# A state space and attention trunk on one core: both mixings reordered, the state space operators on VectorE, small products by turns on column parts

## The chip, the cores and the metric

The kernel runs on one core of one Trainium2 chip. The metric is the device time of one execution in microseconds; three runs of the kernel before are given, and one further execution was taken with the hardware profiler. Engines are named as in the profile: PE (TensorE), with PEld for its weight loads, DVE (VectorE), ACT (ScalarE), POOL (GpSimd) and SP (the queue that issues most DMAs).

## The reference

Two decoder layers over 256 tokens of width 1024, all in float32. Each layer projects the normed tokens with `w_in` into 768 "self" columns and 256 memory queries, mixes them, projects back with `w_out`, and adds a gated MLP with a three-tap causal convolution (1024 to 2 x 2816 to 1024).

- Layer 0 mixes the self columns with a diagonal state space model: 48 groups of 16 channels, 64 complex states each. Discretised operators come from `lambda`, `log_step`, B and C; then GELU, and a sigmoid gate with `w_glu` (768 x 768).
- Layer 1 mixes them by causal attention, 12 heads of 64, over keys and values computed once from the tokens that enter that layer (with 256 tokens the block selection of the reference leaves only the own block).
- In both layers 4 more heads attend without a mask to 256 memory tokens, normed and projected with `w_mem_kv`.

## The kernel before

Activations lie transposed, channels on partitions and the 256 tokens in the free dimension. A weight is loaded by SP in tiles of 128 x 1024 in a fixed list (`Stream`, L64 to L130), then usually split: ACT copies it to a rounded high part (L115), DVE subtracts to get the low part (L119, L121), and each product is three one-pass matmuls (`mm3`, L249 to L251). Weights named in `NATIVE` (L32) are not split; they are multiplied in plain float32. PE executes in program order.

Layer 0 is written as small steps, most of them generators, and a string `ORDER` names them one by one. Inside `manual_schedule` PE, DVE and POOL execute in the order of that string; ACT and SP, and everything after it, are ordered by a scheduler's priorities. In it:

- `P` projects with `w_in` (L869). `rx*`, `rm*` are the norms of tokens and memory: sums of squares on POOL, a power on POOL (L288), a Newton step on DVE.
- `coefficients` (L680 to L745) computes the discretised eigenvalues in many small DVE operations before anything else. `E0`, `E1` raise them to 64 powers in four rounds (piece 0: 8 pairs of groups, on DVE; piece 1: 16 pairs, on POOL).
- The 768 columns are three blocks of 8 pairs. For block b: `Xr`, `Xi` form the input operator (L638: two products of 128 x 512, two sums of 64 x 512), `T`, `t` transpose its halves on PE, `B` copies a part, `V` forms the output operator in three operations of 128 x 1024 (on POOL, L635), `u` scales the projected input, `U` places it by copies (on ACT or DVE, by `U_ACT`).
- `S` is the state recurrence in four steps: products with the input operator on PE (L896, L897), six rotations on DVE, two scans on DVE, then the rotation back into `H` (DVE, partly POOL, L925, L926).
- `l0`, `l1` build the operators inside a chunk on PE (L838, L841), and `L` copies them out. `Y` forms the outputs from both (L941, L944) and transposes them, `G` is GELU.
- `K`, `K1` project the memory for layers 0 and 1 (`mem_kv`, L377, L381). `mkv` of layer 1 is split in three products, and `m` splits the memory tokens for it. `q` scales the memory queries, `A` moves all four memory heads by one stage.

After the string come the gate products with `w_glu`, the gate itself, the output projection and the addition to the tokens (L1079), and then the MLP of layer 0 (`psU`, from 183.07 us of the trace). Layer 1 is ordered by priority throughout; `ORDER1` gives the order in which its steps are issued. A head there is four steps: scores, softmax, transposes, product with the values (L470, L471). The two heads of a pair write the lower and the upper 64 partitions of one bank.

## Time and profile before

| | |
|---|---|
| three runs | 694.43, 694.61, 701.04 us (median 694.61) |
| profiled execution | 695.04 us, of which the span from first to last instruction is 693.3 us |
| busy in the span | PE 654.1 us (94%), DVE 565.4 (82%), ACT 413.2 (60%), POOL 132.9 (19%) |
| mean granted PE clock | 0.957 of 2.4 GHz |
| stages | layer 0 mixing to 183, MLP to 375, layer 1 mixing to 496.7, MLP and final norm to 693.3 us |

PE busy counts an instruction from its start to a modelled end, so neighbours overlap: what one product costs is read from the distance between starts. Plain float32 matmuls show as two records each. A stretch's clock of 0.77 means that PE ran for part of it at 1.2 instead of 2.4 GHz.

### The profile page before, as it was taken

To read this page: it belongs to the slowest core of one execution; us is meant where nothing else is said; L and a number is where in the kernel's file an instruction comes from. 1 tells how busy PE (TensorE), PEld (TensorE's weight loads), DVE (VectorE), ACT (ScalarE), POOL (GpSimd) and SP (SyncE) were. 2 spreads that over 40 slices of the span, in tenths; PEclk is the share of its full clock that TensorE was granted. 3 is DMA by queue.
4 is the path that set the end of the run, shared out by engine and by line. 5 is a ranking of instruction groups with operands and counts; after the bars stand their busy time and mean duration, and the time that the engine had idled before them with its cause. 6 is when DMAs were issued, how large, how long until landed. Compare 5 with 4: busy or idle time off the path is not lost.

```text
span 693.3 us, 12668 instructions
## 1 busy us (share of the span) xinstructions
PE 654.1 (94%) x4904; PEld 616.5 (89%) x4904; DVE 565.4 (82%) x1012; ACT 413.2 (60%) x747; POOL 132.9 (19%) x134
## 2 busy tenths in 40 slices
PE   6369899999999999999999998989999999999995
PEld 5358888998899999999999997868999999999984
DVE  7996999796879998888888798974749999888872
ACT  6368625576556665555557579864636666555631
POOL 5795623402300000000001255500300000000000
PEclk9775879999999999999999999899999999999998
DMA  8610133274455555555555544323625555565401
GB/s 315 245 62 1 61 99 99 93 217 148 152 181 184 183 183 181 186 185 182 182 186 156 168 128 140 107 89 122 213 92 182 181 186 183 183 188 187 172 1 61
DMA packets 43259, 105.13 MB, mean 152 GB/s; under 512 B 3776, under 2 KB 14144, under 8 KB 43200
## 3 DMA queue, kind: packets, MB, share of 16 engines
q1 hardware_dynamic: 42624, 103.74, 45.9%
q8 instruction: 38, 0.62, 0.4%
q10 hardware_dynamic: 576, 0.59, 0.2%
q14 instruction: 21, 0.17, 0.1%
HBM read 103.28 MB, written 1.05 MB: 150 GB/s over the span
## 4 chain that ended last, share of the span: by engine, by line
PE 82%; DVE 12%; DMA 2%; issue 2%; ACT 1%; POOL 0%; SPq 0%; DVEq 0%; ACTq 0%
PE psU L250 12%; PE psU L251 12%; PE psU L249 12%; PE acc L557 9%; PE acc L249 7%; PE acc L250 7%; PE acc L251 7%; PE ps L377 2%; DVE wlo L119 2%; PE ps L381 2%; PE ps L838 1%; DMA s5c<-s5b 1%; PE psO L470 1%; DVE X L638 1%; PE psT L458 1%
## 5 line engine op out<-in xcount | busy, mean ns | idle before, releaser
L115 ACT ACTIVATE whi<-wraw 128x1024 fp32r<-128x1024 f32 (+1 forms) x176 | 182.9, 1042 | 142.4 <-PE psU L250 84.9
L119 DVE TENSOR_TENSOR wlo<-wraw,whi 128x1024 fp32r<-128x1024 f32 (+1 forms) x176 | 217.9, 1240 | 26.7 <-PE acc L251 13.1
L250 PE MATMUL psU<-xlo,whi 128*128 128x256 f32 x704 | 198.6, 282 | 1.4 <-DVE xlo L331 1.4
L251 PE MATMUL psU<-xhi,wlo 128*128 128x256 f32 x704 | 197.8, 282 | 0.0
L249 PE MATMUL psU<-xhi,whi 128*128 128x256 f32 x704 | 197.6, 282 | 0.0
L250 PEld LDWEIGHTS psU<-xlo,whi 128*128 128x128 f32 x704 | 132.9, 189 | 2.5 <-DVE xlo L331 1.8
L249 PEld LDWEIGHTS psU<-xhi,whi 128*128 128x128 f32 x704 | 132.7, 189 | 0.7
L251 PEld LDWEIGHTS psU<-xhi,wlo 128*128 128x128 f32 x704 | 132.6, 189 | 0.0
L528 DVE SCALAR_TENSOR_TENSOR y<-u,held,y 128x254 f32<-128x254 f32 (+1 forms) x176 | 77.8, 477 | 1.5 <-ACT y L526 1.5
L521 DVE TENSOR_TENSOR u<-psU,rb 128x512 f32<-128x512 f32 x44 | 30.3, 688 | 32.4 <-PE psU L251 31.3
L526 ACT ACTIVATE y<-u,held 128x256 f32<-128x256 f32 x88 | 47.6, 589 | 13.0 <-DVE u L521 12.9
L269 POOL TENSOR_TENSOR sq<-sq 128x512 f32<-128x512 f32 x5 | 8.0, 1598 | 226.9 <-DVE held L364 179.1
L251 PE MATMUL acc<-ah,wlo 128*128 128x256 f32 x176 | 49.7, 283 | 0.0
L250 PE MATMUL acc<-al,whi 128*128 128x256 f32 x176 | 49.7, 283 | 0.0
L249 PE MATMUL acc<-ah,whi 128*128 128x256 f32 x176 | 49.6, 282 | 0.0
L869 PE MATMUL acc<-xg,wraw 128*128 128x256 f32 x128 | 34.1, 429 | 5.5 <-ACT xg L859 5.5
L869 PEld LDWEIGHTS acc<-xg,wraw 128*128 128x128 f32 x128 | 27.7, 221 | 10.0 <-ACT xg L859 5.5
L288 POOL TENSOR_TENSOR y<-mf,held 128x1 f32<-128x1 f32 x2 | 1.1, 550 | 180.5 <-DVE mf L1215 180.5
L249 PEld LDWEIGHTS acc<-ah,whi 128*128 128x128 f32 x176 | 33.6, 191 | 0.0
L251 PEld LDWEIGHTS acc<-ah,wlo 128*128 128x128 f32 x176 | 33.5, 191 | 0.0
L250 PEld LDWEIGHTS acc<-al,whi 128*128 128x128 f32 x176 | 33.5, 191 | 0.0
L250 PE MATMUL acc<-xlo,whi 128*128 128x256 f32 x112 | 31.7, 284 | 0.0
(271 smaller groups left out, 1475.1 us busy)
## 6 DMA issues: line engine op xcount, KB each, us to landing
wraw<-w_up SPq DMA_DIRECT2D x88, 512.0 KB, 3.4
wraw<-w_down SPq DMA_DIRECT2D x44, 512.0 KB, 3.4
wraw<-w_out SPq DMA_DIRECT2D x16, 512.0 KB, 3.6
wraw<-w_in SPq DMA_DIRECT2D x15, 512.0 KB, 3.5
wraw<-w_mem_kv SPq DMA_DIRECT2D x8, 512.0 KB, 4.2
wraw<-w_kv SPq DMA_DIRECT2D x6, 512.0 KB, 3.7
wraw<-w_kv SPq DMA_DIRECT2D x8, 384.0 KB, 3.4
wraw<-w_glu SPq DMA_DIRECT2D x6, 384.0 KB, 3.5
```

The lines of the kernel that those rows point to most:

```text
L115: self.nc.scalar.activation(hi[:, c], t[:, c], AF.Copy, scale=1.0 if g_ is None else g_)
L119: self.nc.vector.tensor_sub(lo[:, c], t[:, c], hi[:, c].bitcast(F32))
L249: PE.matmul(out, whi, ahi, start=first, stop=False, skip_group_check=True)
L250: PE.matmul(out, whi, alo, start=False, stop=False, skip_group_check=True)
L251: PE.matmul(out, wlo, ahi, start=False, stop=last, skip_group_check=True)
L377: PE.matmul(pk[:, 256 * m:256 * m + 256], w[i][:, o + 128 * m:o + 128 * m + 128], g[j], start=k + m + i + j == 0, stop=k == KT - 1, skip_g ...
L381: PE.matmul(pv[:, 256 * t:256 * t + 256], g[j][:, 128 * t:128 * t + 128], w[i][:, o + 256:o + 512], start=k + t + i + j == 0, stop=k == KT ...
L521: V.tensor_mul(u, v2(p), rb2(rb))
L526: S.activation(y[:, j], u[:, j], AF.Identity, bias=cp(3), scale=cp(2))
L528: V.scalar_tensor_tensor(y[:, j, d:], u[:, j, :T - d], cp(2 - d), y[:, j, d:], op0=ALU.mult, op1=ALU.add)
L557: PE.matmul(dacc[2 * t + h], a_, w_[:, 512 * i:512 * i + 512], start=False, stop=last and a_ is al, skip_group_check=True)
L869: PE.matmul(acc[2 * h + b][:, 256 * (m % 2):256 * (m % 2) + 256], w[:, 512 * i + 128 * m:512 * i + 128 * m + 128], xg[k // 2][:, k % 2], s ...
```

## The change

1. `V` runs on DVE but for the last of its nine operations (`V_POOL`), all of `H` on DVE, `Xr2` instead of `Xi0` on POOL. The rounds of the powers are shared out singly: POOL has the last of piece 0 and the first three of piece 1. Copies move between ACT and DVE (`U_ACT` leaves 4 of 12 DVE copies, `T_ACT`, `Y_ACT`, `EVAC_ACT`).
2. The state products use 64 columns of weights at a time, lower and upper half by turns (`tile_position`); the chunk operators go round four column parts of 32; the outputs alternate between two of 64; and the two heads of a pair are multiplied with their values by turns, in a step of their own (`p`).
3. `mkv` of layer 1 is native: no low parts, no split memory (`m` is gone), four passes instead of three. The skip term's operands come ready from memory, so the DVE products `dd` go.
4. Both strings are new. Layer 0's has a `|`: what stands behind it (gate, output projection and the addition are steps now: `g`, `g0` to `g2`, `o`, `z`) goes by priority. `P` moves in half steps, softmax in two. The list of weights follows the strings (`by_steps`).

```diff
-NATIVE = (("mkv", 0), ("win", 0))
+NATIVE = (("mkv", 0), ("mkv", 1), ("win", 0))
...
-P rm0 E0 P rx1 E1 P rx2 E0 P rx3 Xi0 Xr0 E0 V1 u0 t0 V0 V0 Xi1 u1 P B0 T0 D0 V0 Xr1 V1 U1 U0 P U0 l0 U0 T1 E1 U0 E1
-E1 Xi2 Xr2 E0 U1 S0 V1 P t2 S0 T2 S0 L0 U1 L0 P B1 L0 V2 t1 S0 D1 u2 U1 V2 U2 U2 U2 m S1 U2 S2 K S1 K K D2 K rm1 V2
-S1 B2 q l1 S1 L1 L1 rm2 L0 S2 Y0 S2 m S2 K K K K rm3 Y0 K L1 L1 G0 m K1 Y1 G0 Y2 Y1 K1 K1 m Y2 K1 G1 G2 K1 K1 G1 K1
-A G2 A A A A K1 A K1 A
+P E0 P P E1 P P P rm0 E0 Xr0 rx1 P P P rx2 E0 rx3 E0 E1 P Xi0 u0 D0 P U0 T0 U0 P U0 t0 P E1 D2 Xr1 P U0 V0 B0 Xi1 S0
+u1 V0 V0 l0 T1 Xi2 U1 S0 P U1 S0 l0 V2 V1 P V1 L0 V2 t1 K Xr2 B1 S0 L0 T2 U1 K u2 V1 rm1 U2 K U2 U1 L0 L0 Y0 B2 K U2
+t2 U2 E1 S1 V2 l1 D1 l1 l1 l1 L1 rm2 L1 S1 rm3 S2 Y0 S1 S1 K L1 K S2 K S2 Y0 L1 S2 K K1 Y1 K G0 G0 | q Y2 Y2 h1 Y1 h2
+Y1 h1 h3 h3 K1 K1 h0 Y2 h2 G1 h1 G2 h0 K1 K1 h0 K1 G1 h2 G2 h3 h1 h2 h0 K1 h3 K1 g g g g g p1 g0 g0 g g1 p0 g1 p1 K1
+g2 p0 o o o o g2 o o o o z3 z2 z1 z0
 """
-X_POOL = ((0, 1),)
-E_POOL = (1,)
-M_POOL = (1, 2, 3)
-H_DVE = (1,)
-V_DVE = ()
-Y_ACT = (0, 1, 2)
-EVAC_ACT = (0, 1, 2)
-T_ACT = ((0, 0), (0, 1), (1, 0), (1, 1), (2, 0), (2, 1))
-U_ACT = ((1, 1, 1, 0), (0, 1, 1, 1), (1, 0, 1, 1))
+V_POOL = ((2, 2),)
+X_POOL = ((2, 0),)
+E_POOL = ((0, 3), (1, 0), (1, 1), (1, 2))
+H_DVE = (0, 1, 2)
+Y_ACT = (1,)
+EVAC_ACT = (0, 2)
+T_ACT = ((0, 0), (0, 1), (1, 1), (2, 0), (2, 1))
+U_ACT = ((1, 1, 1, 0), (1, 1, 1, 1), (1, 1, 1, 1))
 ORDER1 = """
-I I r1 X I I I r2 X I I I r3 Q0 qm Q1 h0 Q2 Q1 h2 K h0 K K X X h3 h2 K h1 R0 h1 h2 K K v v Q0 R1 R0 h3 R1 h0 h4 h5
-h1 h3 v R2 v h7 e0 h10 Q2 h4 h6 h5 h8 h9 h7 h4 v v v h11 R2 v h2 h10 h6 h9 h13 h4 h5 h1 h14 h8 h6 h10 h0 h8 h12 h6
-h7 h12 h3 O h11 h7 h13 h9 h14 h11 e1 h8 h12 h15 h15 h9 h13 h10 h12 h14 h13 h15 h5 h11 O O h15 h14 O O z1 O O O z0 z2
-z3
+x x x x I I I X r1 r2 I I I I r3 I X Q0 qm Q1 K K Q1 h0 K X h3 X h2 Q2 K h1 h0 K h2 h2 R0 h1 h2 v Q0 R1 v R0 h3 R1 v
+h0 h3 h1 K Q2 h10 h7 h0 h1 h5 v R2 h4 h3 h5 h4 h4 h7 v v h8 h5 h4 h11 h6 h10 h9 v v p0 h6 e0 h9 h10 h6 R2 h13 h5 p1 h7
+h8 h14 h8 h7 h8 h12 h6 p1 p0 e1 h10 h9 h12 O h11 p3 h13 h12 h12 h9 h15 h11 p3 h13 h14 h11 h15 h14 p4 p5 h13 h15 p2 p2
+p5 p4 p6 O h14 O h15 p7 p6 p7 O z0 O O O O z3 z2 z1
 """
-ST_DVE = [('k', 1)]
+ST_DVE = (('k', 1), ('q', 0))
...
+    def by_steps(steps, **lists):
+        its = {n: iter(l) for n, l in lists.items()}
+        return [w for s_ in steps.split() if s_ in its for w in next(its[s_], ())]
...
+    order = by_steps(ORDER, P=[w0[:2], []] + [p for w in w0[2:] for p in ([w], [])], K=mkv(0), K1=mkv(1), g=one(glu),
+                     o=one(wout(0)))
+    order += ffn_order(0)
+    order += by_steps(
+        ORDER1, I=one(win(1)),
+        K=one([(("wk", ks, b), blocks(a["w_kv"], ks, 256 * b, 256), (4, 256)) for ks, b in WK]),
+        v=one([(("wv", ks, c), blocks(a["w_kv"], ks, SELF + 384 * c, 384), (2, 384)) for c in range(2) for ks in PAIRS]),
+        O=one(wout(1)))
+    order += ffn_order(1)
...
+                PE.matmul(pk[:, 256 * m:256 * m + 256], w[:, o + 128 * m:o + 128 * m + 128], mk, start=k + m == 0,
+                          stop=k == KT - 1, skip_group_check=True)
...
+                PE.matmul(pv[:, 256 * t:256 * t + 256], mk[:, 128 * t:128 * t + 128], w[:, o + 256:o + 512],
+                          start=k + t == 0, stop=k == KT - 1, skip_group_check=True)
...
-    def pv(out, off, v, PT, causal):
-        c = 128 if causal else 0
-        PE.matmul(out[off:off + 64, :256], v[0], PT[:, 0], start=True, stop=False, skip_group_check=True)
-        PE.matmul(out[off:off + 64, c:256], v[1], PT[:, 1, c:], start=False, stop=True, skip_group_check=True)
-    def head(h, sl, bs, bt, bo, q, k, v, causal, outp, hi, lo):
+    def pv(out, pair, causal):
+        for t in range(2):
+            c = 128 if t and causal else 0
+            for h in range(2):
+                v, PT = pair[h]
+                PE.matmul(out[64 * h:64 * h + 64, c:256], v[t], PT[:, t, c:], start=t == 0, stop=t == 1,
+                          skip_group_check=True)
+    def head(h, sl, bs, bt, q, k, v, causal, outp):
         p = scores(bs, q(h // 4), k(h // 4), h // 2 % 2, h % 2, causal)
         yield
-        P = softmax(sl, p, causal)
+        m = softmax(sl, p, causal)
+        next(m)
         yield
-        PT = transp(sl, bt, P, causal)
+        P = next(m)
         yield
...
+        outp[h] = v(h), transp(sl, bt, P, causal)
         yield
...
+    def head_pair(i, bo, causal, outp, hi, lo):
+        po = bo("psO")
+        pv(po, [outp.pop(2 * i + h) for h in range(2)], causal)
+        yield
+        o = po[:, :256]
+        S.activation(hi[i], o, AF.Copy)
+        V.tensor_sub(lo[i], o, hi[i].bitcast(F32))
+        yield
...
-            op(v[:, :, 1:5], cb[0], ab[0], ALU.mult)
-            yield
-            op(t, cb[1], ab[1], ALU.mult)
-            yield
-            op(v[:, :, 1:5], v[:, :, 1:5], t, ALU.add)
-            yield
+            for r, (o_, a_, b_, f) in enumerate(((v[:, :, 1:5], cb[0], ab[0], ALU.mult), (t, cb[1], ab[1], ALU.mult),
+                                                 (v[:, :, 1:5], v[:, :, 1:5], t, ALU.add))):
+                (gop if (b, r) in V_POOL else vop)(o_, a_, b_, f)
+                yield
         def local_operator(i):
             n, nf = LEN[i], LEN[i] // 4
             Tm[i] = s5.tile([128, n, 4, 32], F32, name=f"Tm{i}")
             G.memset(Tm[i], 0.0)
...
             for f in range(nf):
+                o = [p[32 * s:32 * s + 32, 128 * f:128 * f + 128] for s in range(4)]
+                for g in range(2):
+                    for s in range(4):
+                        PE.matmul(o[s].rearrange("p (i c) -> p i c", c=32)[:, :, 16 * g:16 * g + 16],
+                                  Bz[i][:, 4 * f + s, g], Vd[i][:, 4 * f + s, g, 0:4], start=g == 0, stop=False,
+                                  tile_position=(0, 32 * s), skip_group_check=True)
                 for s in range(4):
-                    pr = 4 * f + s
-                    o = p[32 * s:32 * s + 32, 128 * f:128 * f + 128]
-                    for g in range(2):
-                        PE.matmul(o.rearrange("p (i c) -> p i c", c=32)[:, :, 16 * g:16 * g + 16],
-                                  Bz[i][:, pr, g], Vd[i][:, pr, g, 0:4], start=g == 0, stop=False,
-                                  tile_position=(0, 32 * s), skip_group_check=True)
...
+                    PE.matmul(o[s][:, :32], ident[:, 32 * s:32 * s + 32], dsk[:, PC[i][0] // 4 + f], start=False,
+                              stop=True, tile_position=(0, 32 * s), skip_group_check=True)
+                yield
...
-                if ks != (0,):
-                    yield
+                    if ks != (0,):
+                        yield
...
-                PE.matmul(pr[:, 64 * j:64 * j + 64], RT[b][0][:, j], U[b][:, j], start=True, stop=True)
-                PE.matmul(pi[:, 64 * j:64 * j + 64], RT[b][1][:, j], U[b][:, j], start=True, stop=True)
+                for ri, p in enumerate((pr, pi)):
+                    for c in HALF:
+                        PE.matmul(p[c, 64 * j:64 * j + 64], RT[b][ri][:, j, c], U[b][:, j], start=True, stop=True,
+                                  tile_position=(0, c.start), skip_group_check=True)
...
+            for s in range(4):
+                o = [py[64 * f:64 * f + 64].rearrange("p (i s c) -> p s i c", s=4, c=32)[:, s] for f in range(2)]
+                for f in range(2):
+                    PE.matmul(o[f], U[b][:, 4 * f + s], Tm[pc][:, off + 4 * f + s], start=s == 0, stop=False,
+                              tile_position=(0, 64 * f), skip_group_check=True)
+                for g in range(2):
+                    for f in range(2):
+                        PE.matmul(o[f][:, :, 16 * g:16 * g + 16], Hs[b][:, 4 * f + s, g],
+                                  Vd[pc][:, off + 4 * f + s, g, 1:5], start=False, stop=True,
+                                  tile_position=(0, 64 * f), skip_group_check=True)
             yield
...
+        def gate():
+            d["g"] = [ba("acc") for _ in range(3)]
+            for ks, b in GLU:
+                gemm(d["g"], ("glu", ks, b), ks, lambda k: [yp[k // 2][i][:, k % 2] for i in range(2)], 2 * b, 2,
+                     ks[0] == 0, ks[0] == 3)
                 yield
+        def gated(b):
+            t = sx([128, 2, T], name="gt")
+            S.activation(t, v2(d["g"][b]), AF.Tanh, scale=0.25)
+            V.scalar_tensor_tensor(t, t, 1.0, yT[b], op0=ALU.add, op1=ALU.mult)
+            yield
...
+        def output0():
+            d["o"] = [ba("acc") for _ in range(4)]
+            yield from gemm_halves(d["o"], "wout", 0, WOUT[0], lambda k: (moh[k - 6], mol[k - 6]) if k >= 6 else
+                                   (oh[k // 2][:, k % 2], ol[k // 2][:, k % 2]))
...
+        by_hand, by_priority = ORDER.split("|")
+        with tc.manual_schedule(engines=MANUAL):
+            steps(by_hand)
+        steps(by_priority)
...
+        for i in range(2):
+            gens[f"p{i}"] = head_pair(i, bank(2), False, outm, ohi[6:], olo[6:])
+        for i in range(6):
+            gens[f"p{2 + i}"] = head_pair(i, bank(5), True, outq, ohi, olo)
```

## Rows read from the trace of the kernel before

**Rows 1.** The page: the span, and PE's granted clock in 40 equal slices.

```profile
span 693.3 us, 12668 instructions
...
PEclk9775879999999999999999999899999999999998
```

**Rows 2.** Busy time by stage: length, PE, PEld, DVE, ACT, POOL; clock, DMA share, GB/s.

```profile
24.00:118.90 94.90, 76.99 (x477) 67.06 (x478) 86.99 (x127) 52.11 (x126) 56.57 (x60) 0.77 0.22 70
118.90:183.00 64.10, 64.10 (x557) 61.15 (x556) 49.48 (x73) 41.54 (x74) 15.92 (x16) 1.00 0.49 160
183.00:190.00 7.00, 5.84 (x49) 5.64 (x49) 7.00 (x9) 4.04 (x7) 3.32 (x3) 1.00 0.41 125
...
418.00:460.00 42.00, 36.31 (x211) 31.08 (x209) 36.96 (x71) 34.90 (x82) 18.16 (x17) 0.88 0.39 128
```

**Rows 3.** Who waited for whom, PE, 0 to 200 us: total, times, longest.

```profile
PE ps L771 <- DVE X L638: 11.8, 1, 11.8
```

**Rows 4.** DVE in order of time: start, length of the merged row.

```profile
32.01 4.62 DVE L638 TENSOR_TENSOR X<-xt 64x512 f32<-64x512 f32 x2
36.66 2.26 DVE L638 TENSOR_TENSOR ee<-E 128x16 f32<-128x16 f32 x1
...
44.18 1.44 DVE L638 TENSOR_TENSOR X<-xt 64x512 f32<-64x512 f32 x2
...
58.34 0.19 DVE L638 TENSOR_TENSOR ee<-E 128x16 f32<-128x16 f32 x1
```

**Rows 5.** POOL in order of time.

```profile
36.16 2.72 POOL L635 TENSOR_TENSOR Vd<-Vd,vt 128x1024 f32<-128x1024 f32 x1
```

**Rows 6.** DVE groups, 24 to 118.9 us: count, busy us, mean ns, idle before.

```profile
L888 DVE COPY U<-uT 32x128 f32<-32x128 f32 x12 | 6.8, 563 | 0.3
...
L121 DVE SCALAR_TENSOR_TENSOR wlo<-wraw,held,whi 128x512 fp32r<-128x512 f32 x4 | 6.0, 1526 | 0.0
...
L903 DVE TENSOR_TENSOR rot<-ps,E 128x512 f32<-128x512 f32 x3 | 2.1, 685 | 4.9 <-PE ps L896 4.9
```

**Rows 7.** DVE groups, 118.9 to 190 us.

```profile
L119 DVE TENSOR_TENSOR wlo<-wraw,whi 128x1024 fp32r<-128x1024 f32 x14 | 17.4, 1246 | 4.8 <-ACT ks L415 1.5 <-PE acc L251 1.4 <-PE ps L381 0.8
```

**Rows 8.** POOL groups, 24 to 118.9 us.

```profile
L635 POOL TENSOR_TENSOR Vd<-Vd,vt 128x1024 f32<-128x1024 f32 x3 | 7.9, 2639 | 0.0
L635 POOL TENSOR_TENSOR Vd<-s5c 128x1024 f32<-128x1024 f32 x3 | 7.0, 2356 | 0.1
L926 POOL TENSOR_TENSOR H<-rot 64x504 f32<-64x504 f32 x4 | 6.3, 1580 | 11.6 <-DVE rot L920 11.5
L635 POOL TENSOR_TENSOR vt<-s5c 128x1024 f32<-128x1024 f32 x3 | 6.2, 2080 | 0.2
```

**Rows 9.** PE in order of time, layer 0.

```profile
43.63 3.62 PE L869 MATMUL acc<-xg,wraw 128*128 128x256 f32 x16
...
80.42 0.39 PE L897 MATMUL ps<-U,RT 128*128 128x64 f32 x2
80.64 0.39 PE L896 MATMUL ps<-U,RT 128*128 128x64 f32 x2
...
101.10 0.41 PE L838 MATMUL ps<-Vd,Bz 128*32 128x64 f32 x4
...
101.61 0.41 PE L838 MATMUL ps<-Vd,Bz 128*32 128x64 f32 x4
...
109.92 0.22 PE L944 MATMUL psY<-Vd,H 128*64 128x64 f32 x1
109.92 0.32 PE L941 MATMUL psY<-Tm,U 128*64 128x128 f32 x1
```

**Rows 10.** PE in order of time, layer 1's value products.

```profile
468.39 0.65 PE L470 MATMUL psO<-PT,vv 128*64 128x256 f32 x2
...
473.75 0.66 PE L470 MATMUL psO<-PT,vv 128*64 128x256 f32 x4
```

**Rows 11.** The chain that ended last: one-pass products of 512 columns.

```profile
669.25 16.78 PE acc L557 x72
```

More of the change, by code (lines that the diff above doesn't have):

```diff
@@ L364, in residual, with mem_kv @@
                 V.scalar_tensor_tensor(xs, accs[b], scale, xs, op0=ALU.mult, op1=ALU.add)
-    def mem_kv(l, bk, mh, ml, ks, new, vm):
+    def mem_kv(l, bk, mem, ks, new, vm):
         pk, pv = bk(), bk()
@@ L370, in mem_kv @@
             if k % 2 == 0:
-                w = W.get(("mkv", l, k // 2))
-            o = 512 * (k % 2)
-            g = [m if m is None else m[k // 2][:, k % 2] for m in (mh, ml)]
-            pairs = [(i, j) for i, j in ((0, 0), (0, 1), (1, 0)) if w[i] is not None and g[j] is not None]
+                w, _ = W.get(("mkv", l, k // 2))
+            o, mk = 512 * (k % 2), mem[k // 2][:, k % 2]
             for m in range(2):
-                for i, j in pairs:
-                    PE.matmul(pk[:, 256 * m:256 * m + 256], w[i][:, o + 128 * m:o + 128 * m + 128], g[j],
-                              start=k + m + i + j == 0, stop=k == KT - 1, skip_group_check=True)
+                PE.matmul(pk[:, 256 * m:256 * m + 256], w[:, o + 128 * m:o + 128 * m + 128], mk, start=k + m == 0,
+                          stop=k == KT - 1, skip_group_check=True)
             for t in range(2):
-                for i, j in pairs:
-                    PE.matmul(pv[:, 256 * t:256 * t + 256], g[j][:, 128 * t:128 * t + 128],
-                              w[i][:, o + 256:o + 512], start=k + t + i + j == 0, stop=k == KT - 1,
-                              skip_group_check=True)
+                PE.matmul(pv[:, 256 * t:256 * t + 256], mk[:, 128 * t:128 * t + 128], w[:, o + 256:o + 512],
+                          start=k + t == 0, stop=k == KT - 1, skip_group_check=True)
             yield
@@ L776, in transpose_input_operator, with powers @@
                     V.tensor_copy(o, p)
-        def powers(i, op):
+        def powers(i):
             e, n = E[i], LEN[i]
-            for c, up, down in ((2, 1, 0), (6, 1, 2), (14, 7, 6), (42, 21, 20)):
+            for r, (c, up, down) in enumerate(((2, 1, 0), (6, 1, 2), (14, 7, 6), (42, 21, 20))):
+                op = gop if (i, r) in E_POOL else vop
                 h = e[:, :, :, c // 2]
@@ L992, in layer0 @@
         acc = [ba("acc") for _ in range(4)]
-        gens = {"P": project(acc), "K": mem_kv(0, bw, memT, None, ks, st, vm),
-                "K1": mem_kv(1, bw, mh, ml, ks1, lambda *_: next(st1), vm1),
-                "E0": powers(0, gop if 0 in E_POOL else vop), "E1": powers(1, gop if 1 in E_POOL else vop),
-                "A": attend([head(h, sq, br, bw, bw, lambda i: qs, lambda i: ks, values_of(vm), False, outp, moh, mol)
-                             for h in range(4)])}
+        gens = {"P": project(acc), "K": mem_kv(0, bw, memT, ks, st, vm),
+                "K1": mem_kv(1, bw, memT, ks1, lambda *_: next(st1), vm1), "E0": powers(0), "E1": powers(1),
+                }
+        for h in range(4):
+            gens[f"h{h}"] = head(h, sq, br, bw, lambda i: qs, lambda i: ks, values_of(vm), False, outp)
+        for i in range(2):
+            gens[f"p{i}"] = head_pair(i, bw, False, outp, moh, mol)
         for b in range(3):
@@ L1050, in layer0, with steps @@
                 calls[f"{n}{b}"] = lambda f=f, b=b: f(b)
+        gens["g"], gens["o"] = gate(), output0()
+        for b in range(3):
+            gens[f"g{b}"] = gated(b)
+        for b in range(4):
+            calls[f"z{b}"] = lambda b=b: residual0(b)
         for i in range(2):
-            calls[f"l{i}"] = lambda i=i: local_operator(i)
+            gens[f"l{i}"] = local_operator(i)
             gens[f"L{i}"] = put_local_operator(i)
-        with tc.manual_schedule(engines=MANUAL):
-            for s in ORDER.split():
+        def steps(text):
+            for s in text.split():
                 if s in gens:
@@ L1091, in layer1 @@
         causal_ops.extend([identb, maskb])
-        act, d = split_x(1), {}
+        sq_, d = [], {}
+        act = split_x(1, steps=sq_)
         rb = pool.tile([128, T], F32, name="rbq")
```

117 lines of the change are left out of this document (30 added, 87 removed).

## The prediction

> **What bounds the kernel now.** The page first: the low digits of PE's granted clock lie in the first seven slices, with one 8 about slice 25 and one at the very end [rows 1]. PE is the engine with most work, so time can be won where it waits or runs slowly. The stage table gives the sizes [rows 2]. From 24.0 us (where the coefficients end) to 118.9 us (where DVE finishes the last step of the third `S`), PE is busy 77.0 of 94.9 us, at a clock of 0.77, while DVE is busy 87.0 of 94.9. From 118.9 to 183.0, where the MLP begins, PE is busy for all of 64.1 us at full clock. So the first stretch is DVE's, the second is PE's. The two MLPs are full on PE and untouched. Layer 1's mixing is full on PE too, except from 418 to 460 us: 36.3 of 42 us at a clock of 0.88.
>
> The list of waits shows how DVE holds PE: 11.8 us at once for the first input operator [rows 3]. Then look at DVE's operations in order of time. An operation of 16 columns (`ee`) takes 2.26 us at 36.66 us and 0.19 us at 58.34; two halves of `X` take 4.62 us at 32.0 and 1.44 at 44.2 [rows 4]. At 36.16 us POOL runs one of the `V` operations for 2.72 us [rows 5], and the slow `ee` ends when that does. DVE is standing in front of something that POOL holds. I set each DVE group of the stretch against its undisturbed duration (0.72 us for 512 columns by the fast `X` halves, 0.19 for `ee`, and so on); the largest single excess is that of the four half tiles of `wlo`, 4 x (1.53 - 0.72) = 3.2 us [rows 4, 6]. Over some fifteen groups I get **24.0 us of delay in DVE's 87.0**; 63.0 us are work. POOL was busy 56.6 us meanwhile, 21.1 of them `V` and 6.3 `H` [rows 2, 8].
>
> **First stretch, DVE's sum.** Taken away: two low part tiles of `mkv`, 4 x 0.72 = 2.9 us; `m` and `dd`, 2.1 (estimate at undisturbed length); `q` moved behind the bar, 2.1; eight `U` copies at about 0.5, 4.0 [rows 6]. Together 11.1. Added: eight `V` operations of 1024 columns; DVE's operation of that size is the split, 1.25 us with some delay in it [rows 7], so I take 1.2, 9.6 us in all. The four halves of `H` from POOL, 4 x 0.68, 2.7; two copies of transposes and one of outputs, 1.8; the round of powers that comes less the one that goes, 1.1. Together 15.2. DVE's work is then 63.0 - 11.1 + 15.2 = 67.1 us. `Xr2` for `Xi0` is even.
>
> Delay: POOL loses eight of nine `V` operations (21.1 - 2.6 = 18.5), `H` (6.3), one subtraction for `m` (1.3) and some 3 of powers, so 56.6 falls to about 27.4 us. At the old rate, 24.0/56.6 = 0.42 us of DVE delay for each us of POOL, 11.6 us remain. Bounds: 4 us, if POOL's rest lies beside DVE operations that read PSUM (the first rotations, `L903`, took 0.685 us on the mean with POOL at work beside the first of them [rows 6]); and 27 us, if all of it holds DVE. I take 11.6, the rate of the rows. Idle: DVE stood 7.9 us, 4.9 of them for the first state products [rows 6], which PE could reach only after `l0`; in the new string `S0` stands ahead of `l0`. Bounds 3 and 8, I take 5.
>
> So the third `S` ends at 24.0 + 67.1 + 11.6 + 5 = 107.7 us, **11.2 us sooner**. PE must keep up. At full clock its old work there takes less than 77.0 us, and it loses there. A group of chunk products and skip term repeats every 0.51 us at full clock, 24 of them 12.3 us [rows 9]. By turns on four column parts it should take half or less: where the old outputs pass from one column part to the other, two products start in the same hundredth of a microsecond [rows 9], and where layer 1's value products of two heads happen to lie side by side, four records take 0.66 us as two do alone [rows 10]. So 5 to 6 us go. The state products, 48 at 0.22 us [rows 9], gain between nothing (if loading 128 columns of weights in two halves takes as long) and half; I take 3 of 10.7. Against it `Y1` (2 us after turns) and one step of `K1` (1.7) come in from the second stretch. About 72 us of PE in 83.7 then: PE hides under DVE, without much to spare.
>
> **Second stretch, PE's sum.** It was 64.1 us of PE without a gap. `Y1` moves ahead of it (8 x 0.455 = 3.65 us by the outputs' own spacing), since `S1` now ends well before `S2`: -3.65. `Y2` by turns: from 3.65 to 2.2 (0.6 of it, as the one overlap in the rows suggests), -1.45. Four memory heads' value products side by side instead of one by one: eight products of 0.43, half of it saved, -1.7. `K1` native: a plain product takes 3.62/8 = 0.45 us less the tail of the last, 0.43 between starts [rows 9], so 32 of them 13.9; before, 96 passes at 0.117 (half of 16.78/72 for 512 columns [rows 11]), 11.3. So +2.6; one of its eight steps lies earlier, -1.7. DVE has work here too (the weights' low parts, GELU, softmax), but was busy only 49.5 of 64.1, and loses the other two low part tiles. The new danger is the gate, which stands in a queue of its own behind `G2`; with heads and `K1` between to fill, I add 1. Sum: 64.1 - 3.65 - 1.45 - 1.7 + 2.6 - 1.7 + 1 = 59.2 us. The MLP begins at 107.7 + 59.2 = 166.9 instead of 183.1: **-16.2 us**. DVE is full from 183 to 190 before and after (the addition, the split of the tokens), so that corner stays.
>
> **Layer 1.** The gap between 418 and 460 us is worth 5.7 us of idle and, by the clock of 0.88, at most 5 more. For it: value products always by pairs (three pairs of heads that lay apart, 0.8 us each, 2.4 us), softmax's multiplication in its own step, one stack of queries off POOL, statistics sooner. Against it: three more steps between a head's scores and its use, so that a buffer stays taken longer, and 1.4 us more on DVE, which was busy 37.0 of 42. I take -4, bounds -9 and +3. Following the weights' list by use and the half steps of `P` I cost at nothing: weights are loaded ahead and PE's order holds the same products; a load that came late would cost PE a wait such as the list of waits does not show now.
>
> The sum: 695.04 - 16.2 - 4 = 674.8 us for the profiled execution, which lies 0.4 above the median; so **674 us**.
>
> **The rivals.** *More than that.* The new string lays POOL's rest out of DVE's way: delay 4, idle 3, the third `S` ends at 98, the MLP begins at 157, layer 1 gives 9: about 660. For it speaks that the operations POOL keeps are short; against, that the powers work only on SBUF, as DVE's `X`, `V` and scans do.
>
> *POOL's rest holds DVE for all its time.* Delay 27 and idle 8: the third `S` ends at 24 + 67.1 + 35 = 126.1, later than now, the MLP begins at 185, and with layer 1's 4 the time is 693, no change. The break-even is plain: delay and idle together may be 33 us, and were 31.9. For it speak [rows 4, 5], where the wait lasted as long as POOL's operation; against, that less than half of POOL's time turned into delay. The Trainium skill, in "SBUF — State Buffer", section "SBUF: two separate sides", says that VectorE operations with two SBUF inputs and GpSimd operations that read SBUF lock one shared pair of ports for the whole instruction, the loser blocking fully. The slow `ee` agrees with that; moving `V` to DVE does not end the lock, it adds eight more operations that want it.
>
> *The turns bring nothing.* If parts of the array load and multiply one after the other, `Y2` and the pairs lose their 3.2 us, and PE's work in the first stretch rises to some 80 of 83.7 us, which would delay DVE's chain by about 4: 681.
>
> *Slower.* PE falls to 1.2 GHz for good in the first stretch: shorter, more scattered products leave it idle more often. Its work there at full clock is about 55 us (half of `P` is done by 24 us); at a mean clock of 0.5 that is 110 us, the third `S` ends at 134, the MLP begins at 193, and with -4 from layer 1 the time is 701. It decides below a clock of 55/83.7 = 0.66; the old string had 0.77 with PE idle for 18 us [rows 2].
>
> **How the numbers follow.** Forecast 0.50 (665 to 684 by half of each bound), more 0.20, POOL holds DVE 0.14, turns bring nothing 0.10, slower 0.06. To leave out no more than 2 in 10 the range must reach from the case above 660 to about 690: 657 to 690. A change under 1% (7 us) can't be told from none here. Faster by more: 0.50 + 0.20 + 0.10 and a fifth of the POOL case, 0.83; slower by more, most of the last case and a little of the POOL case, 0.06; the rest 0.11.
>
> **What would show it.** In the profile after: `V` on DVE at 1.2 us each; the third `S` over near 108 us with DVE over 90% busy up to there; PE full from there to an MLP that starts near 167 us; state products at 0.22 us or less, chunk operators in a quarter to a half of their time; `K1` at 1.73 us a step. The forecast is wrong if DVE's small operations are as slow as before beside POOL's powers, if PE shows gaps after 108 us before the gate's products, or if layer 1's stretch of low clock has grown.

## The result, and the profile after

The changed kernel takes 671.23 us (median of 4 runs, 669.97 to 672.11), the kernel before 694.83 us on the same chip (4 runs, 694.43 to 701.04): a ratio of 0.9639, 95% interval 0.9582 to 0.9696. The profiled execution took 671.97 us. Runs of the kernel before fall near 694.5 or near 700 us, and every ratio carries that spread; the variants are therefore compared with the changed kernel by their own medians and by marks in their traces.

The page first: span, PE and POOL busy in the whole span, PE's granted clock by slices, to be read against [rows 1].

```profile
span 670.2 us, 12678 instructions
...
PE 629.2 (94%) x4968; PEld 595.2 (89%) x4968; DVE 547.5 (82%) x1011; ACT 408.0 (61%) x746; POOL 103.7 (15%) x117
...
PEclk9799698899999999999999997999999999999998
```

The low digits of the first seven slices are fewer, and one low digit stays in layer 1. Now the stage table, with the columns of [rows 2]: up to the end of the third `S`, from there to the first MLP, the MLP's first 7 us, and layer 1's mixing.

```profile
24.00:105.50 81.50, 66.75 (x688) 57.42 (x687) 75.18 (x119) 51.74 (x130) 36.48 (x49) 0.90 0.25 83
105.50:165.50 60.00, 55.42 (x424) 51.78 (x425) 47.88 (x73) 38.70 (x69) 12.65 (x10) 0.91 0.50 174
165.50:172.50 7.00, 7.00 (x60) 6.93 (x59) 6.32 (x11) 4.77 (x8) 2.23 (x2) 1.00 0.01 2
...
354.80:472.40 117.60, 113.32 (x867) 106.60 (x866) 97.68 (x185) 88.89 (x199) 32.60 (x27) 0.96 0.39 129
```

By these marks the first MLP begins 17.6 us sooner (165.5 for 183.1). Layer 1's first projection starts at 354.86 instead of 375.0, so another 2.5 us lie in the first MLP's stretch. The second MLP begins at 472.4 instead of 496.7: 4.2 more for layer 1. The rest is 197.8 us long for 196.6.

The waits of PE, 0 to 200 us (columns as in [rows 3], whose 11.8 us for `X` is gone):

```profile
PE psY L943 <- DVE H L925: 10.3, 3, 8.4
PE acc L866 <- ACT xg L856: 5.5, 1, 5.5
PE ps L286 <- POOL sq L282: 4.8, 2, 3.4
PE psS L431 <- DVE qs L412: 3.0, 1, 3.0
PE ps L834 <- DVE Vd L642: 2.7, 1, 2.7
```

PE still waits for DVE in the first stretch, but inside one place, the first outputs. What DVE does just then, and POOL beside it, each in order of time:

```profile
53.21 0.69 DVE L902 TENSOR_TENSOR rot<-ps,E 128x512 f32<-128x512 f32 x1
...
55.61 0.68 DVE L906 TENSOR_TENSOR rot<-rot 128x512 f32<-128x512 f32 x1
56.21 1.76 DVE L907 TENSOR_TENSOR rot<-rot 128x512 f32<-128x512 f32 x1
57.89 2.28 DVE L910 TENSOR_TENSOR_SCAN rot<-dec,rot 128x512 f32<-128x512 f32 x1
60.10 2.22 DVE L911 TENSOR_TENSOR_SCAN rot<-dec,rot 128x512 f32<-128x512 f32 x1
62.24 2.33 DVE L642 TENSOR_TENSOR Vd<-s5c 128x1024 f32<-128x1024 f32 x2
...
69.74 0.68 DVE L917 TENSOR_TENSOR rot<-rot,E 128x512 f32<-128x512 f32 x1
...
52.71 2.96 POOL L639 TENSOR_TENSOR X<-xt 64x512 f32<-64x512 f32 x2
...
55.93 1.49 POOL L280 TENSOR_TENSOR sq<-sq 128x512 f32<-128x512 f32 x1
57.38 1.71 POOL L281 TENSOR_TENSOR sq<-sq 128x512 f32<-128x512 f32 x1
59.17 2.06 POOL L282 TENSOR_TENSOR sq<-sq 128x512 f32<-128x512 f32 x1
...
69.21 1.79 POOL L828 MEMSET Tm<- 128x2048 f32 x1
```

As in [rows 4, 5], a DVE operation with both inputs in SBUF is long where POOL reads SBUF too: a scan takes 2.2 us here and 1.2 us in the second and third block, where POOL is idle; L907 takes 1.76 us, while its neighbour of the same size, which began before POOL's, takes 0.68. It is not long wherever POOL works: the rotations that read PSUM (from 53.21 us) keep 0.68 us each beside POOL's `X`, and L917 keeps it beside a POOL operation that only writes (`MEMSET`). `V` costs 1.2 us on DVE (two records in 2.33).

The rest of PE's order in time: one block's state products, the chunk operators, the outputs. They answer [rows 9].

```profile
80.73 2.09 PE L895 MATMUL ps<-U,RT 128*64 128x64 f32 x64
82.75 0.43 PE L834 MATMUL ps<-Vd,Bz 128*32 128x64 f32 x16
...
83.06 0.41 PE L834 MATMUL ps<-Vd,Bz 128*32 128x64 f32 x16
...
105.67 0.39 PE L939 MATMUL psY<-Tm,U 128*64 128x128 f32 x4
105.89 0.40 PE L943 MATMUL psY<-Vd,H 128*64 128x64 f32 x8
106.12 0.39 PE L939 MATMUL psY<-Tm,U 128*64 128x128 f32 x4
```

Four pairs of chunk operators now repeat every 0.3 us instead of 4 x 0.51; a block's state products take 2.1 us instead of 16 x 0.22 = 3.5; two pairs of outputs repeat every 0.455 us, which one pair took before (its spacing in the prediction).

### The profile page after: what moved, and what is told of

Its sections match the earlier page's. It is cut to its first block, busy times and chain, and to the rows that moved or that the text cites. A ratio compares the mean times of both kernels' runs of the same rounds, so it can differ in the third digit from the quotient of the medians.

```text
span 670.2 us, 12678 instructions
## 1 busy us (share of the span) xinstructions
PE 629.2 (94%) x4968; PEld 595.2 (89%) x4968; DVE 547.5 (82%) x1011; ACT 408.0 (61%) x746; POOL 103.7 (15%) x117
## 4 chain that ended last, share of the span: by engine, by line
PE 76%; DVE 18%; ACT 2%; issue 2%; DMA 0%; POOL 0%; DVEq 0%; ACTq 0%
PE psU L262 13%; PE psU L260 12%; PE psU L261 12%; PE acc L562 9%; PE acc L261 7%; PE acc L262 7%; PE acc L260 7%; DVE wlo L119 2%; DVE X L642 1%; PE psO L481 1%; DVE xt L642 1%; PE ps L388 1%; DVE cf L649 1%; DVE Vd L642 1%; PE psT L465 1%
## 5 line engine op out<-in xcount | busy, mean ns | idle before, releaser
L119 DVE TENSOR_TENSOR wlo<-wraw,whi 128x1024 fp32r<-128x1024 f32 (+1 forms) x176 | 212.8, 1212 | 31.2 <-PE psU L262 14.9
L262 PE MATMUL acc<-xhi,wlo 128*128 128x256 f32 x112 | 31.6, 283 | 0.0
```

The source lines that it names most:

```text
L119: self.nc.vector.tensor_sub(lo[:, c], t[:, c], hi[:, c].bitcast(F32))
L262: PE.matmul(out, wlo, ahi, start=False, stop=last, skip_group_check=True)
```

## Experiments

Eight kernels start from the changed one, four from the one before (where a string is exchanged, its steps are translated to the new sizes). Beside the medians stand marks of the trace: the end of the third `S` and the start of layer 1's first projection, in the changed kernel 105.5 and 354.9 us, in the one before 118.9 and 375.0. A mark comes from one execution. How far marks scatter shows in the kernel with layer 1's old order: its layer 0 is the changed one, yet the third `S` ends at 106.2 us and the first MLP begins at 163.4, 2.1 us sooner. Differences of this size are not read from marks alone.

### `V` back on POOL

```diff
-V_POOL = ((2, 2),)
+V_POOL = tuple((b, r) for b in range(3) for r in range(3))
```

> The changed kernel with all nine output operator operations on POOL again, as before the change; the strings stay. Theory A (the sum of the prediction): what POOL does costs DVE 0.42 us per us, so eight operations back on POOL (18.5 us) cost DVE 7.8 us of delay and free 9.6 us of its work; moving them was about even and the gain came from elsewhere: 668 to 675 us, as the changed kernel (671). Theory B (the lock is what the change was about): nearly all of the 18.5 us delay DVE, which is the bound up to 105 us, and POOL's queue makes DVE wait for the powers: 680 us or more.

676.0 us (674.94 to 676.59), ratio 0.969 [0.9636, 0.9744], between the two theories; third `S` 114.4, layer 1 at 360.0. DVE's busy time is what my arithmetic made it, 73.0 us for 75.2. But its idle time rises from 6.3 to 17.4 us, and the waits of 24 to 114.4 us, of PE and of DVE, say why:

```profile
PE ps L834 <- POOL Vd L639: 7.1, 1, 7.1
...
DVE RT L780 <- PE ps L775: 11.5, 1, 11.5
```

The chunk operators stand in PE's order and wait for `V`, which comes late through POOL's queue; the transposes that DVE needs stand behind them. **DVE's busy time is no reason for the move: it pays by latency.**

### `V` and `H` on DVE in the kernel before, nothing else

```diff
-H_DVE = (1,)
-V_DVE = ()
+H_DVE = (0, 1, 2)
+V_DVE = (0, 1, 2)
```

> The kernel before with one part of the change alone: all output operator operations and all of the last rotation's sums on DVE, in the old string. Theory A (0.42 us of delay per us of POOL): DVE gets 10.8 + 2.7 us more work and loses 27.4 x 0.42 = 11.5 us of delay: 692 to 699 us, no change. Theory B (the lock): 27.4 us of delay go for 13.5 us of work: 685 us or less.

706.0 us (703.72 to 706.48), ratio 1.0115 [1.0057, 1.0173]: **about 1% slower**, outside both theories. In its profiled execution the third `S` ends at 128.4 and layer 1 begins at 384.6; DVE is busy 89.5 us of 104.4, 2.5 more than in the one execution of before that was profiled, and 7 us more idle. The queues show again: PE waits 11.4 us for the skip term's operand, which DVE makes at 54.4 us, 51.0 in the kernel before (`PE ps L841 <- DVE dd L829`, a wait of 4.1 us before). In the old string the same move is a loss.

### No turns

The old sequence of state products, chunk operators, outputs and value products (one head's two, then the other's) in the changed kernel.

```diff
-                for ri, p in enumerate((pr, pi)):
-                    for c in HALF:
-                        PE.matmul(p[c, 64 * j:64 * j + 64], RT[b][ri][:, j, c], ...
+                PE.matmul(pr[:, 64 * j:64 * j + 64], RT[b][0][:, j], U[b][:, j], start=True, stop=True)
+                PE.matmul(pi[:, 64 * j:64 * j + 64], RT[b][1][:, j], U[b][:, j], start=True, stop=True)
...
```

> The changed kernel with the old sequence of small products: state products 128 columns wide, chunk operators one pair after the other, outputs first one column part and then the other, value products one head after the other. All else stays. The chunk operators took 0.42 us for four pairs after the change where 2.06 us would be the old spacing; over states, chunk operators and outputs PE saved about 17 us at full clock. Theory A: PE hides under DVE in the first stretch, so only what lies behind the third state recurrence counts, and some of the first stretch where PE stands ahead of DVE: 674 to 679 us. Theory B (the turns carry the gain in layer 0): 683 us or more.

674.02 us (672.38 to 674.74), ratio 0.9655 [0.959, 0.9721]: 2.8 us, theory A at its lower edge. The third `S` ends at 109.9, 4.4 later, all of it DVE's idle time (11.1 us for 6.3; `DVE rot L899 <- PE ps L892` is 4.7 us, and 1.2 with turns). The stretch behind it is 57.4 us long for 60.0, at a clock of 1.00 for 0.91, and layer 1 begins at 356.7, 1.8 later; layer 1 takes 117.0 us, no more than with turns. PE's timeline without them, three steps of the state products and of the chunk operators:

```profile
86.54 0.39 PE L893 MATMUL ps<-U,RT 128*128 128x64 f32 x2
86.76 0.39 PE L892 MATMUL ps<-U,RT 128*128 128x64 f32 x2
...
87.58 0.30 PE L834 MATMUL ps<-Vd,Bz 128*32 128x64 f32 x4
87.69 0.22 PE L837 MATMUL ps<-dsk,held 128*32 128x32 f32 x2
87.72 0.30 PE L834 MATMUL ps<-Vd,Bz 128*32 128x64 f32 x4
87.83 0.22 PE L837 MATMUL ps<-dsk,held 128*32 128x32 f32 x2
87.86 0.30 PE L834 MATMUL ps<-Vd,Bz 128*32 128x64 f32 x4
```

The state products are back at 0.22 us each. But a pair of chunk operators repeats every 0.14 us, without any turns, where it took 0.51 [rows 9]. So most of that fall is not the turns': it is the other thing that changed there, the skip term, now a product of the form 128*32 with its operand ready from memory, where it was 32*32 (this row of the kernel before lies between those of [rows 9], which show the 0.51 from start to start):

```profile
101.44 0.24 PE L841 MATMUL ps<-dd,held 32*32 32x32 f32 x2
```

Turns halve the 0.14 again (0.29 for four).

### Turns and ready operands alone, in the kernel before

The same edit the other way round, and the skip term's operands ready from memory.

> The kernel before with one part alone: state products, chunk operators and outputs by turns on column parts, and the skip operands ready from memory (no dd on DVE). In the old string PE stands in front of DVE at 47 to 66 us (chunk operators of piece 0 at half clock, 6.6 us, then state products 6.8) and again at 99 to 120 us. Theory A (what the turns save counts only where PE is ahead of DVE): 6 to 10 us at the first place and 6 to 8 at the second: 677 to 684 us. Theory C (DVE's sum sets the pace anyway, as the changed kernel without turns, at 674, suggests): 689 to 694 us.

691.41 us (690.95 to 693.95), ratio 0.9908 [0.9882, 0.9934], as theory C says; third `S` about 118.1, layer 1 at 371.2. PE is busy 60.8 us up to the third `S` instead of 77.0, and it ends 0.8 us sooner: DVE sets the pace there. Some 3 us come behind it, where the outputs are PE's own.

### Layer 1's old order of steps

```diff
-x x x x I I I X r1 r2 I I I I r3 I X Q0 qm Q1 K K Q1 h0 K X h3 X h2 Q2 ...
+x x x x I I r1 X I I I r2 X I I I r3 Q0 qm Q1 h0 Q2 Q1 h2 K h0 h0 K K ...
```

> The changed kernel with layer 1's steps issued in the old order (softmax's two halves next to each other, the pair's product where the second head's stood). Layer 1's mixing took 117.5 us after the change and 121.8 before. Theory A: the order gave most of it: 674 to 677 us. Theory B: the pairing of value products and the stack of queries on DVE gave it, the order nothing: 670 to 673 us.

670.37 us (669.71 to 672.58), ratio 0.9616 [0.9561, 0.9672]; layer 1 takes 117.9 us for 117.5, as theory B says. The new `ORDER1` gives nothing on balance, but the two orders are not alike inside. Here are the second stretch and layer 1 of this kernel:

```profile
106.20:163.40 57.20, 52.45 (x424) 49.28 (x425) 48.49 (x74) 39.04 (x69) 12.69 (x10) 0.97 0.56 187
352.70:470.60 117.90, 109.51 (x862) 102.48 (x861) 94.69 (x184) 88.51 (x197) 31.17 (x27) 1.00 0.43 139
```

In layer 1 PE has the full clock, 1.00 for the changed kernel's 0.96, and is busy 109.5 us for 113.3; it is idle 8.4 us for 4.3. The new order saves idle time, and about as much goes to 10 us at 1.2 GHz (409.7 to 419.9 us). Whether the order itself brings the clock down was not tried.

### Layer 0's old string, all reworked parts kept

```diff
-P E0 P P E1 P P P rm0 E0 Xr0 rx1 P P P rx2 E0 rx3 E0 E1 P Xi0 u0 D0 P U0 T0 U0 ...
+P P rm0 E0 P P rx1 E1 P P rx2 E0 P P rx3 Xi0 Xr0 E0 V1 u0 t0 V0 V0 Xi1 u1 P P ...
...
```

> The changed kernel with layer 0's old string (P in two halves next to each other, chunk operators and outputs in their finer steps next to each other, softmax too; m left out; gate, output projection and addition behind the bar). The placement of operators, the turns and the native weights stay new. Theory A (the new string is what pays: operators on DVE and turns make things even at best): 682 to 692 us. Theory D (the reworked parts carry the gain, the string little): 671 to 677 us.

688.98 us (688.35 to 690.01), ratio 0.9879 [0.9832, 0.9925], as theory A says. Nearly 18 of the 24 us hang on the new string, and few of them in the first stretch: the third `S` ends at 108.8, so the reworked parts alone bring 10 of its 13 us. The first MLP begins at 176.1, and layer 1 at 372.2, hardly sooner than before. The stage table of this kernel, up to the third `S`, to the first MLP, and the MLP's first 7 us, and PE's wait there:

```profile
24.00:108.80 84.80, 62.43 (x604) 54.16 (x603) 78.78 (x132) 52.83 (x132) 33.70 (x49) 0.82 0.22 76
108.80:176.10 67.30, 61.78 (x511) 57.14 (x509) 44.73 (x69) 38.88 (x68) 9.56 (x11) 0.97 0.54 177
176.10:183.10 7.00, 2.67 (x13) 2.47 (x14) 7.00 (x14) 5.75 (x12) 4.05 (x2) 0.71 0.42 126
...
PE psU L261 <- DVE xlo L342: 4.3, 1, 4.3
```

Against the changed kernel's marks, 3.3 us are lost up to the third `S`, 7.3 from there to the MLP, and 6.8 in the MLP's stretch (196.1 us for 189.4). Most of the 7.3 are PE's work: 57 of the 128 records of the memory's projection (`K`, `K1`) lie behind the third `S` here, 28 in the changed kernel, and 29 at 0.215 us are 6.2 us. The first 84.8 us hold 62.4 us of PE although its clock is lower. The 6.8 show at the MLP's start: there DVE is full with the addition and the splits of tokens and weights, PE is busy 2.67 of 7 us, and it waits 4.3 us at once for the tokens' low part (`xlo`). In the changed kernel PE is busy for all of its first 7 us. So the old string gives back what was won on DVE at two places, and only one of them is the memory's projection.

### Four steps of `K` late

```diff
-... V1 L0 V2 t1 K Xr2 B1 S0 L0 T2 U1 K u2 V1 rm1 U2 K U2 U1 L0 L0 Y0 B2 K U2 ...
+... V1 L0 V2 t1 Xr2 B1 S0 L0 T2 U1 u2 V1 rm1 U2 U2 U1 L0 L0 Y0 B2 U2 ... K K K K K K1 Y1
```

> The changed kernel, with the first four steps of the memory's projection (K) taken from beside VectorE's stretch to the place behind the last K of the string's hand-ordered part. Theory A (the new string pays because PE does the memory products while VectorE sets the pace): about 14 products of 0.43 us, 6 us of PE, come back behind the third S, and the time rises by 5 to 7 us, to 676 to 678. Rival (behind the third S PE is not the limit either: in the changed kernel it is idle for 4.6 of 60 us there, at a clock of 0.91): the products fill those holes and the time stays at 670 to 673.

679.1 us (675.23 to 679.83), ratio 0.9716 [0.9679, 0.9754]: **theory A**, slightly above its band by the median; the profiled span grows by 6.5 us. The third `S` ends only 0.8 us later (106.3); the stretch behind it grows by 3.7:

```profile
24.00:106.30 82.30, 62.94 (x619) 54.96 (x620) 74.67 (x122) 51.55 (x131) 34.25 (x49) 0.83 0.23 73
106.30:170.00 63.70, 58.44 (x497) 54.14 (x496) 47.88 (x73) 39.89 (x70) 11.75 (x10) 0.97 0.49 167
```

43 records of memory products lie behind the third `S` for 28; 15 at 0.215 us are 3.2 us, and PE's busy time there grows by 3.0. I had expected all four steps to come back; half found room by DVE's end. The stretch's holes did not take them up: they are waits for DVE and ACT in PE's order. In the first stretch the clock falls to 0.83, almost without cost, as DVE sets the pace there and PE has fewer products. Another 1.4 us between there and layer 1 and 1.1 in layer 1 have no cause that I can show.

### Three steps of `K` earlier

```diff
-... U2 U1 L0 L0 Y0 B2 K U2 ... S1 S1 K L1 K S2 K S2 Y0 L1 ...
+... U2 U1 L0 L0 K K K Y0 B2 K U2 ... S1 S1 L1 S2 S2 Y0 L1 ...
```

> The changed kernel, with three more K steps moved ahead of the first output step Y0, into the 8.4 us in which PE waits there for VectorE's H. Theory A (PE's work behind the third S sets when the MLP begins): the time falls by 2 to 4 us, to 667 to 669. Rival (behind the third S the chain of queries, softmax and GELU on VectorE and ScalarE sets it): no change, 670 to 672.

672.65 us (671.87 to 673.23), ratio 0.963 [0.9592, 0.9667]: as the rival says, but **the run does not tell the two apart**. 28 records lie behind the third `S`, as many as in the changed kernel: the three steps were inside DVE's stretch already, and went from one hole of PE to another. The wait for `H` falls from 10.3 to 6.5 us, and PE waits 6.2 instead of 3.0 for the scaled queries. DVE was also 3.5 us late at 59.75 us, before the first step that I moved: the list of weights follows the string, and ACT's order may follow it; what made DVE late was not traced further.

### The two heads' value products apart

```diff
+        if h ^ 1 in outp:
+            o = outp[h // 2, "po"] = bo("psO")
+            pv(o, h ^ 1, outp.pop(h ^ 1), causal)
...
-        po = bo("psO")
-        pv(po, [outp.pop(2 * i + h) for h in range(2)], causal)
+        po = outp.pop((i, "po"))
+        for h in (2 * i, 2 * i + 1):
+            if h in outp:
+                pv(po, h, outp.pop(h), causal)
```

> The changed kernel, with the value products of the two heads of a pair at different steps again: the first head's ahead of the second's transposes, the second's in the step p. Theory A (products side by side give layer 1 its 2.6 us less of PE, and 1.7 in layer 0): 673 to 676. Rival (layer 1's gain is the order of steps, or waits that end elsewhere): 670 to 672.

681.9 us (680.85 to 682.36), ratio 0.9761 [0.9726, 0.9795]: theory A's sign, at more than twice its size. The first MLP begins 3.3 us later, and layer 1 takes 124.7 us for 117.5. PE's timeline, here, in the kernel without turns and in the changed kernel:

```profile
456.46 0.86 PE L481 MATMUL psO<-PT,vv 128*64 128x256 f32 x4
```

```profile
456.14 0.88 PE L481 MATMUL psO<-PT,vv 128*64 128x256 f32 x8
```

```profile
454.81 0.87 PE L481 MATMUL psO<-PT,vv 128*64 128x256 f32 x8
```

Two products of one head (four records) take as long as the four of both heads, even where these are not by turns: what counts is that the other half's products stand next to them. PE is busy 3.4 us more in layer 1 (116.71 for 113.32) and idle 3.9 us more, mostly waits for softmax (`PE psT L465 <- DVE P L458`, 4.0 for 2.1 us). This is not the layout of before either, where five of eight pairs happened to be adjacent; so the run shows the price of keeping heads apart, not the gain of the change.

### POOL off the scans

Three steps of `K` earlier as above, and the last `V` and the memory's sums of squares on DVE.

```diff
-V_POOL = ((2, 2),)
+V_POOL = ()
...
-            d["pm"] = sums(d["sm"], ba)
+            d["pm"] = sums(d["sm"], ba, V)
```

> The run with three K steps moved ahead of Y0, and also the last V operation and the memory's sums of squares on VectorE instead of POOL: this takes away POOL's long operations beside the scans of S (3.2 us of delay in the changed kernel) and beside one more VectorE operation (1.8 us), and adds 3.2 us of work to VectorE. Theory A (delay beside POOL is real time of VectorE's stretch): 1 to 2 us below the run with the three K steps alone. Rival (the delay falls into VectorE's idle time, or the added work costs as much): the same as that run or slower.

678.88 us (678.18 to 679.62), ratio 0.972 [0.9686, 0.9754]: slower, which the rival allows, but not for its reason. The scans can't tell, because they take 1.2 us already in the run with the three K steps alone: there POOL's sums lie beside rotations that read PSUM, and the scans come after them. What does go is the delay of L907 (1.76 to 0.68 us) and of L916 (2.48 to 0.68), and the first block's last `H` starts at 68.5 us, 73.6 in the changed kernel and 75.1 with the K steps alone. Then the sums stand in DVE's queue behind that `H`, PE's product for the memory's norm stands in front of everything else, and both engines stop in turn. PE, then DVE, in order of time:

```profile
58.77 1.03 PE L388 MATMUL ps<-wraw,memT 128*128 128x256 f32 x4
73.15 1.84 PE L286 MATMUL ps<-held,sq 128*128 128x1 f32 x8 [13.35 <-DVE ee L642]
...
79.38 0.16 DVE L305 SCALAR_TENSOR_TENSOR y<-t,y 128x2 f32<-128x2 f32 x1
90.79 0.69 DVE L902 TENSOR_TENSOR rot<-ps,E 128x512 f32<-128x512 f32 x1 [11.24 <-PE ps L895]
```

Against the changed kernel DVE is 5 us ahead at 69 us and 8 us behind at the third `S` (113.5). Whether the delay is real time once the sums are placed sooner stays open; it was not tried.

### `K1` native alone, in the kernel before

```diff
-NATIVE = (("mkv", 0), ("win", 0))
+NATIVE = (("mkv", 0), ("mkv", 1), ("win", 0))
```

> The kernel before with one part of the change alone: the memory weights of layer 1 native (four passes instead of three, no low parts, no split memory tokens; the steps m are taken out of the string). Theory A (the prediction's terms): PE gets 2.6 us more where it is the bound, behind the third state recurrence; DVE loses 3.6 us of work and about 3 of delay ahead of it: 691 to 695 us. Theory C (the DVE work that the change drops is what shortens layer 0): 685 to 690 us.

702.32 us (700.04 to 703.98, ten runs; the kernel before on that chip 694.23 to 702.51), ratio 1.0048 [1.0015, 1.008]: half a per cent slower, outside both theories. In its profiled execution the third `S` ends no later (118.3 us), and from there to the MLP PE is busy 69.0 us for 64.1, at a clock of 0.98 for 1.00; the MLP begins at 189.8, 6.7 later. The 2.6 us that I had counted for it are right in sign and too small by this one trace.

### The stack of queries on DVE, in the kernel before

```diff
-ST_DVE = [('k', 1)]
+ST_DVE = [('k', 1), ('q', 0)]
```

> The kernel before with one stack of queries of layer 1 (q, 0) on DVE instead of POOL, all else old. Layer 1's mixing took 121.8 us before, 117.5 after, 117.9 with the old order of its steps and 117.0 without the turns, so neither of those two gave the 4 us. Theory A: this stack did: layer 1 117 to 119 us, in all 690 to 692. Theory E: the separate steps of softmax and of the pairs' product did: no change, 694 to 696 us.

695.0 us (691.95 to 700.8), ratio 0.9987 [0.9949, 1.0025]: no change, as theory E says; layer 1 takes 121.1 us for 121.7.

## Why the prediction was right

**The bound.** DVE sets the pace up to the third `S`, PE behind it: right. With turns alone, in the old string, the first stretch moves by 0.8 us; four steps of `K` taken out of the new one leave it 0.8 us longer, and about half of them come back behind it. PE is not free there, though: without turns DVE is idle there for 4.7 us more.

**First stretch.** 107.7 us was forecast, 105.5 came: DVE busy 78.7 forecast, 75.2 measured, idle 5 and 6.3. Set against the shortest record of the same operation in any run, some 9 of the 75.2 are delay, against 11.6 forecast. That term came near by two errors: POOL was busy 36.5 us, not 27.4, and the rate was 0.25 us for each us of POOL, not 0.42. One price was wrong, with little harm: a `U` copy takes 0.24 us (`L885`), so of the 0.563 of [rows 6] more than half was delay, and of the 0.5 that I took about half. By the same measure the delay before was 28 us beside 56.6 of POOL, not 24.0, a rate of 0.49; so the rate fell by half. The rival in which POOL's rest holds DVE for all its time failed with that. The slow scans still bear out the lock that the Trainium skill describes in "SBUF — State Buffer", section "SBUF: two separate sides", for two SBUF inputs; over the whole stretch a quarter of POOL's time, not all of it, is lost. The lower bound that I gave (POOL beside DVE operations that read PSUM) is real too: those rotations keep 0.68 us.

**`V` on DVE.** My own terms made this step a small loss for DVE, 9.6 us of work against 18.5 x 0.42 = 7.8 of delay, and the experiments agree (2.2 us more busy). What it pays by, `V` being there when PE reaches the chunk operators, stood nowhere in the sum. It is worth 4.8 us in the new string and costs 1.15% in the old one together with `H`.

**PE in the first stretch.** "About 72 us, without much to spare" was right in its conclusion and pessimistic in its terms: 66.75 us with far more memory products in it. Chunk operators went to a seventh, where I took half or less; state products gave 1.4 us a block, 4 in all, where I took 3. I had given the chunk operators' gain to the turns and costed the skip term for DVE alone (`dd`); the run without turns shows that its shape on PE was the larger price, 0.37 of the 0.51 us. The rival in which the turns bring nothing expected 681; without them the time is 674, so even that fall would have cost 3 us, not 7. Its 4 us of delay for DVE do come (4.4). Its 3.2 us for `Y2` and the pairs do not: at a like clock the second stretch is 57.4 us long without turns and 57.2 with them (the kernel with layer 1's old order), though PE is busy 55.5 us for 52.5. PE's clock did not fall to 1.2 GHz for good, as the slower rival feared: 0.90 after 0.77.

**Second stretch.** 59.2 us forecast, 60.0 measured, from other terms. It is not full: PE is busy 55.4 us at a clock of 0.91, and by the prediction's own sign (gaps after 108 us ahead of the gate's products) this part failed. The wait that I put at the gate (1 us) is 3.0 us at the memory's scores, behind the queries' scaling, which moved behind the bar (`PE psS L431 <- DVE qs L412`). DVE's two `qs` there take 2.75 us while POOL splits the keys; that this is the same delay was read, not tried. The clock stood nowhere in the sum either: before, this stretch had 1.00; now PE runs at 1.2 GHz from 112.7 to 123.0 us, beginning within that wait. The kernel with layer 1's old order has the same layer 0, a clock of 0.97 there, PE busy for 52.5 us, and a second stretch of 57.2 us, so some 3 of the 60.0 us go with the clock. Against it, 100 of the 128 records of memory products lie ahead of the third `S`. I had moved one step of `K1`, 8 records; of its 64 records 36 are ahead. The other 28 at 0.215 us are 6.0 us that I had left in the second stretch. So this step's sum was right by errors of opposite sign, which is luck. The string that I had treated as a list of small shifts is the largest single part: with the old one the time is 689.

**First MLP's corner.** I had said that the corner with DVE full stays, and put it at nothing. Its first 7 us now have PE busy for all 7.00 us, 5.84 before, and the stretch up to layer 1 is 2.5 us shorter. This term failed. The corner goes with the order of steps: with layer 0's old string PE waits 4.3 us there for `xlo`, and the stretch is 196.1 us long for 189.4. Which of the steps decides it was not tried.

**Layer 1.** -4 forecast, -4.2 measured, and PE's busy time fell by 2.6 at the same clock (0.96), near the 2.4 that I gave to the pairs. Neither the new order (0.4 us on balance) nor the stack of queries (0.6 us in the kernel before) accounts for more. Heads kept apart cost 7 us, 3.4 of it PE. That the pairs are the cause of the 2.6 agrees with the 0.87 us of both heads against 0.86 of one; their share of the idle time that went (5.8 to 4.3 us) is not settled.

## What to carry to other kernels

An engine's share of a stretch tells which engine sets the pace; whether a move pays is then decided by who stands behind the result in which queue, so cost a moved step by its latency as well as by its busy time. When a faster engine shortens its stretch, fill the other engine's holes there with work from behind, or the gain is given back: here four steps moved out of them cost 7.9 us. Then look at the seam to the next stage: with the old string as much was lost at the MLP's start, in DVE's queue, as behind the third `S`. Put products that write different column parts next to each other, keep the number of partitions the same between them, and then see whether turns add anything.

## What the runs showed of the hardware

- Four records of value products on 64 columns take 0.86 us, and eight on both halves 0.87; turns between the halves add nothing to adjacency (0.88 without). Small products gain: state products as halves of 64 columns by turns take 2.1 us a block, 3.5 as whole 128; chunk operators by turns 0.07 us a pair, 0.14 one pair after the other.
- One product over 32 partitions between products over 128 made a pair of chunk operators take 0.51 us; with all three over 128 it takes 0.14. Whether the change of shape or the product itself costs that was not separated.
- A copy of 32 x 128 takes 0.24 us on DVE where the group before showed 0.56: a group's mean can be more than half delay.
- Beside POOL operations that read SBUF, DVE operations with both inputs in SBUF grow (512 columns from 0.68 to 1.76 us, a scan from 1.2 to 2.2); rotations that read PSUM keep 0.68 us, and so does L917 beside a POOL `MEMSET`.
- With four steps of `K` taken out, the granted clock of the first stretch is 0.83 instead of 0.90, and the stretch is only 0.8 us longer: here, where DVE sets the pace and PE has 15 records fewer, the clock hardly tells. In the second stretch it does: 57.2 us at 0.97, 60.0 at 0.91.
